# Rotary angles on GpSimd, a new order of the first loads, and the first token tile's latents ahead of the last transposes

## The chip, the cores and the metric

The kernel runs on one core of a Trainium2 chip. The metric is the device time of one execution, in microseconds (us); lower is better. The core has five engines that work in parallel, each through its own queue in order: PE (TensorE, matrix products), DVE (VectorE), ACT (ScalarE), POOL (GpSimd) and SP (SyncE, which here only issues transfers). Transfers between the chip's main memory and the on-chip memory are done by 16 DMA engines.

## The reference

One layer of a decoder block with 512 tokens of width 1024, all in float32. The normed tokens go through one wide projection, whose first columns are two low-rank latents and a rotary key; the rest feeds a differential attention and two gates.

```python
xn = rmsnorm(x, norm_mix_g[l])
proj = jnp.einsum('bsd,de->bse', xn, w_in[l])
q_lat, kv_lat, k_rope, dq, dk, dv, gate_pre = jnp.split(proj, split_idx, axis=-1)
q = jnp.einsum('bsr,re->bse', rmsnorm(q_lat, mla_q_norm_g[l]), mla_w_uq[l])
...
kv = jnp.einsum('bsr,re->bse', rmsnorm(kv_lat, mla_kv_norm_g[l]), mla_w_ukv[l])
...
o_mla = causal_attention(q_mla, k_mla, v_mla).reshape(B, S, MLA_WIDTH)
...
o_diff = rmsnorm(o1 - lam * o2, diff_subln_g[l]) * (1.0 - lambda_init)
...
x = x + jnp.einsum('bsd,de->bse', merged, w_out[l])
hn = rmsnorm(x, norm_ffn_g[l])
hid = jax.nn.silu(jnp.einsum('bsd,df->bsf', hn, w_ffn_gate[l])) * jnp.einsum('bsd,df->bsf', hn, w_ffn_up[l])
x = x + jnp.einsum('bsf,fd->bsd', hid, w_ffn_down[l])
```

Rotary turns pairs of columns by an angle, position times frequency, so a table of cosines and sines is needed for the 512 positions. The query latent has 384 columns, the other latent 256, the rotary key 32.

## The kernel before

**Two halves.** Every operand of a matrix product is split into a rounded high half and a low half (the rest), and each product is made of three (`mm3`, L298 to L302): high by high, high by low, low by high. High halves are mostly written by ACT, low halves by DVE or POOL.

**The start.** Tokens lie in four tiles x0 to x3 of 128 tokens. `LOADS` gives the order in which SP issues the first transfers: `r` small rows (gains and biases), `x0` a token tile in two column halves, `A0` a pair of query-latent weight tiles (128x384 each), `B0` a pair of tiles of the other latent with the rotary key (128x288 each), `i` the frequency column and the positions. Eight transfers can be in flight; the ninth waits for the first to land. `START` gives the order in which the preparing work is written: `r` turns the small rows into columns, `t0` transposes token tile 0 on PE (L346) and writes its gained halves (`X`, ACT L352, DVE L354), `t23` does tiles 2 and 3 together, `d6` puts six idle products on PE, `a0` and `b0` split a weight tile (L329 to L332; `W_DVE` names the tiles whose high half DVE writes in place of ACT, `W_POOL` those whose low half POOL writes in place of DVE), `s0` sums the squares of a token tile on ACT (L358).

**The latents.** `latent(0)` makes the query latents of all four token tiles, 24 products of 128x384 for each, then `latent(1)` the others, 24 of 128x288. A product tile goes from its bank (three of the kind `ps_mm`) through ACT, which squares and copies it (L448, L450). Between the third and the fourth tile of `latent(1)` stand the products that make the rotary tables (L539), from the angles.

**The angles.** L397 to L416 work out position times frequency, reduced to one turn in five steps, on DVE, on tiles of 128x128 and 128x256. Their result is `turn`; ACT makes its absolute value and eight sines (L419, L428), DVE splits those (L431, L432).

**Behind the start** come the gates, the projections of attention, the attention heads (a score step L632, a maximum on DVE L636, an exponential on ACT, transposes L658, values), the output and the FFN. Weights there go through `weights`: a raw tile (four buffers), a high half by `round_hi`, a low half by `round_lo` on the engines in `w_eng`, which is `W_ENG0` up to the first attention head's stage and `W_ENG` after it.

**What sets the order.** The program is written in one order; a scheduler then places each engine's instructions by priorities and its own model of the time, with `issue_after` as a way to hold one behind another. So a change at the start can move instructions far behind it.

Of the kernel before, what the change touches and what calls it, by code (L numbers as in the profile page):

```python
# [21 lines left out]
P = 128  # L22
# [70 lines left out]
def build(ctx, nc, tc, a, out):  # L93
# [29 lines left out]

    def dma(o, i):
        nc.sync.dma_start(out=o, in_=i)
# [21 lines left out]
    table = [nc.scalar.preload_act_table_set(LOG_EXP)]  # L147
# [24 lines left out]
    def load_x(t):  # L172
        for c in range(2):
            dma(xts[t][:, c * S:(c + 1) * S], a["x"][0, t * P:(t + 1) * P, c * S:(c + 1) * S])
# [29 lines left out]

    for step in LOADS:
        k = int(step[1:] or 0)
        if step[0] == "x":
            load_x(k)
# [49 lines left out]

    w_eng = list(W_ENG0)

    def round_hi(o, i):
        if w_eng[0] == 'act':
            nc.scalar.activation(out=o, in_=i, func=AF.Copy)  # L263
        else:
            nc.vector.tensor_copy(out=o, in_=i)  # L265
# [56 lines left out]
    last_t, last_hi = [None], [None]  # L322

    def latent_weights(b, k):
# [5 lines left out]
        else:  # L330
            nc.scalar.activation(out=w[:, 0, :], in_=raw, func=AF.Copy)
# [6 lines left out]
    def scaled_transpose(t0, t1):  # L338

        n = t1 - t0  # L340
        for k0 in range(0, KD, 4 // n):
# [11 lines left out]
            for src, hi, lo, g in parts:  # L353
                nc.vector.scalar_tensor_tensor(out=lo, in0=src, scalar=g, in1=r32(hi), op0=ALU.mult, op1=ALU.subtract)  # L354

    def x_square(t):
        with tc.issue_after(last_hi[0].ins):
            nc.scalar.activation(out=xts[t], in_=xts[t], func=AF.Square, accum_out=x_ss[:, t:t + 1])  # L358

    for step in START:  # L360
# [6 lines left out]
        elif step[0] in "ab":  # L367
            latent_weights("ab".index(step[0]), k)
        else:
            if step[0] == "s":  # L370
                x_square(k)
            else:
                scaled_transpose(k, int(step[-1]) + 1)
# [3 lines left out]

    def xa(k, sl=slice(None)):
        return [xn[k // 4][:, k % 4, s, sl] for s in range(2)]
# [6 lines left out]
    nc.vector.tensor_mul(out=lp, in0=lv[:, 0:4:2, :], in1=lv[:, 1:4:2, :])  # L386
# [14 lines left out]
    nc.vector.tensor_copy(out=ahl[:, 0, :], in_=r32(ah))  # L401
    nc.vector.tensor_sub(out=ahl[:, 1, :], in0=ang, in1=ahl[:, 0, :])
    for j, c in enumerate(_inv_2pi_pieces()):
        nc.vector.tensor_scalar(out=ry, in0=ahl, scalar1=c, scalar2=MAGIC, op0=ALU.mult, op1=ALU.add)
        nc.vector.tensor_scalar(out=ry, in0=ry, scalar1=MAGIC, scalar2=0.0, op0=ALU.subtract, op1=ALU.add)
        nc.vector.tensor_scalar(out=rx, in0=ahl, scalar1=c, scalar2=0.0, op0=ALU.mult, op1=ALU.add)
        if j == 0:
            nc.vector.tensor_sub(out=acc, in0=rx, in1=ry)
        else:
            nc.vector.tensor_sub(out=rx, in0=rx, in1=ry)  # L410
            nc.vector.tensor_add(out=acc, in0=acc, in1=rx)
    nc.vector.tensor_add(out=turn, in0=acc[:, 0, :], in1=acc[:, 1, :])
    for _ in range(2):
        nc.vector.tensor_scalar(out=ry[:, 0, :], in0=turn, scalar1=MAGIC, scalar2=0.0, op0=ALU.add, op1=ALU.add)
# [583 lines left out]
```

## Time and profile before

| what | us |
|---|---|
| median of 3 runs (764.81 to 767.35) | 766.11 |
| the profiled execution | 765.69 |
| its span in the profile | 763.9 |
| DVE busy in the span | 430.5 |
| ACT busy in the span | 293.4 |
| POOL busy in the span | 166.9 |

The profile is of one execution. A row of a timeline has the start and the length in us, the engine, the line of the kernel, the operation, what it writes and reads by the program's names, the shape, a count where equal instructions follow each other, and in brackets how long the engine stood idle before it and what ended that. Rows of a table by stretch have the stretch, its length, the busy us of PE, of PE's weight loads, of DVE, ACT and POOL, then PE's granted clock, the share of the DMA engines and GB/s.

### The profile page before, as it was taken

What the parts mean: (1) busy time and instruction counts of PE and PEld (TensorE: products, weight loads), DVE (VectorE), ACT (ScalarE), POOL (GpSimd) and SP (SyncE); (2) the same over time, 40 slices, a digit from 0 to 9 for tenths busy, and PEclk for the clock granted to TensorE, in tenths of its full rate; (3) what the DMA queues carried; (4) which work ended last, traced back from release to release, by engine and by line L of the source; (5) the groups of instructions that cost most, each with busy time, mean ns of one, the idle gap of its engine ahead of it and who ended that gap; (6) DMA issues with size and microseconds to landing.
All of it is one profiled execution on the core that took longest, in us unless ns stands there. A gap on an engine that the chain in (4) does not pass through costs nothing.

```text
span 763.9 us, 9613 instructions
## 1 busy us (share of the span) xinstructions
PE 738.9 (97%) x3639; PEld 620.5 (81%) x3639; DVE 430.5 (56%) x800; ACT 293.4 (38%) x567; POOL 166.9 (22%) x120
## 2 busy tenths in 40 slices
PE   7999999999898999999999999999999999999996
PEld 5888889887686788888889888888888888888885
DVE  6968698898999983578363333233323332213424
ACT  7464658554333421724243323222222223122314
POOL 3404343564664454430000000000000000000302
PEclk9999999999999999999999999999999999999999
DMA  9405343632422322327422332323232323232302
GB/s 305 113 1 133 88 122 88 151 85 58 108 70 69 84 83 82 111 87 254 102 83 73 94 110 83 110 83 111 83 110 83 111 83 110 85 108 84 111 0 110
DMA packets 99819, 76.72 MB, mean 100 GB/s; under 512 B 6303, under 2 KB 86973, under 8 KB 99773
## 3 DMA queue, kind: packets, MB, share of 16 engines
q1 hardware_dynamic: 99773, 76.12, 34.0%
q8 instruction: 28, 0.46, 0.2%
q14 instruction: 18, 0.15, 0.1%
HBM read 69.81 MB, written 2.10 MB: 94 GB/s over the span
## 4 chain that ended last, share of the span: by engine, by line
PE 80%; DVE 13%; issue 2%; ACT 1%; POOL 1%; DMA 1%; SPq 0%; DVEq 0%; POOLq 0%; ACTq 0%
PE ps_mm L301 22%; PE ps_mm L302 22%; PE ps_mm L300 22%; PE ps_sc L632 2%; DVE L L256 2%; PE ps_sc L300 1%; PE ps_sc L301 1%; PE ps_tr L301 1%; PE ps_tr L300 1%; PE ps_tr L302 1%; PE ps_sc L302 1%; DVE L L254 1%; PE ps_tr L658 1%; DVE w L265 1%; DVE P L684 1%
## 5 line engine op out<-in xcount | busy, mean ns | idle before, releaser
L302 PE MATMUL ps_mm<-X,w 128*128 128x512 f32 (+1 forms) x568 | 217.6, 383 | 0.0
L300 PE MATMUL ps_mm<-X,w 128*128 128x512 f32 (+1 forms) x568 | 217.3, 383 | 0.2 <-DVE t L564 0.2
L301 PE MATMUL ps_mm<-X,w 128*128 128x512 f32 (+1 forms) x568 | 217.3, 383 | 0.0
L268 DVE TENSOR_TENSOR w<-raw,w 128x1024 fp32r<-128x1024 f32 x66 | 82.3, 1248 | 161.1 <-ACT w L263 161.0
L263 ACT ACTIVATE w<-raw 128x1024 fp32r<-128x1024 f32 (+1 forms) x72 | 74.0, 1029 | 160.1 <-issue 78.9
L268 POOL TENSOR_TENSOR w<-raw,w 128x1024 fp32r<-128x1024 f32 (+3 forms) x48 | 102.5, 2139 | 118.3 <-DVE w L265 36.3
L300 PEld LDWEIGHTS ps_mm<-X,w 128*128 128x128 f32 x568 | 107.1, 189 | 20.3 <-DVE t L564 0.4
L301 PEld LDWEIGHTS ps_mm<-X,w 128*128 128x128 f32 x568 | 107.2, 189 | 19.9 <-DVE X L254 0.2
L302 PEld LDWEIGHTS ps_mm<-X,w 128*128 128x128 f32 x568 | 107.1, 189 | 20.0 <-POOL w L268 0.3
L933 POOL TENSOR_TENSOR L<-L,P 128x512 f32<-128x512 f32 (+1 forms) x9 | 11.5, 1297 | 410.2 <-ACT t L932 410.1
L155 ACT ACTIVATE P<-P,sm 128x128 f32<-128x128 f32 (+3 forms) x64 | 35.9, 561 | 60.1 <-DVE sm L636 59.9
L907 DVE TENSOR_TENSOR t<-t,ps_mm 128x512 f32<-128x512 f32 x22 | 15.1, 688 | 59.7 <-PE ps_mm L302 59.7
L632 PE MATMUL ps_sc<-L,L 96*128 96x128 f32 (+7 forms) x160 | 38.0, 334 | 8.7 <-DVE sm L636 8.6
L906 ACT ACTIVATE t<-ps_mm 128x512 f32<-128x512 f32 x22 | 13.2, 598 | 80.8 <-PE ps_mm L302 80.8
L632 PEld LDWEIGHTS ps_sc<-L,L 96*128 96x128 f32 (+1 forms) x160 | 26.1, 191 | 14.6 <-DVE sm L636 12.3
L301 PE MATMUL ps_mm<-w,L 128*128 128x512 f32 (+1 forms) x100 | 37.2, 372 | 0.0
L300 PE MATMUL ps_mm<-w,L 128*128 128x512 f32 (+1 forms) x100 | 37.2, 374 | 0.0
L302 PE MATMUL ps_mm<-w,L 128*128 128x512 f32 (+1 forms) x100 | 37.1, 373 | 0.0
L265 DVE CAST w<-raw 128x1024 fp32r<-128x1024 f32 (+3 forms) x42 | 35.9, 855 | 1.6 <-PE ps_mm L302 1.1
L250 ACT ACTIVATE L<-t 64x512 fp32r<-64x512 f32 (+2 forms) x47 | 29.1, 624 | 17.0 <-POOL t L566 7.4
L301 PE MATMUL ps_mm<-L,w 128*128 128x512 f32 x90 | 35.5, 394 | 0.0
L254 DVE TENSOR_TENSOR L<-t,L 128x512 fp32r<-128x512 f32 (+2 forms) x37 | 33.1, 896 | 4.0 <-ACT L L250 3.7
(264 smaller groups left out, 1269.0 us busy)
## 6 DMA issues: line engine op xcount, KB each, us to landing
raw<-w_in SPq DMA_DIRECT2D x28, 512.0 KB, 4.0
raw<-w_ffn_gate SPq DMA_DIRECT2D x22, 512.0 KB, 3.9
raw<-w_ffn_up SPq DMA_DIRECT2D x22, 512.0 KB, 3.9
raw<-w_ffn_down SPq DMA_DIRECT2D x22, 512.0 KB, 3.6
L<-L SPq DMA_DIRECT2D x32, 128.0 KB, 2.3
raw<-w_out SPq DMA_DIRECT2D x8, 512.0 KB, 3.6
L<-x SPq DMA_DIRECT2D x8, 256.0 KB, 5.1
raw<-w_branch_mla SPq DMA_DIRECT2D x4, 512.0 KB, 3.4
```

The source lines that it names most:

```text
L155: return nc.scalar.activation(**kw)
L250: nc.scalar.activation(out=hi, in_=src, func=AF.Copy, scale=scale)
L254: nc.vector.tensor_sub(out=lo, in0=src, in1=r32(hi))
L256: nc.vector.scalar_tensor_tensor(out=lo, in0=src, scalar=scale, in1=r32(hi), op0=ALU.mult, op1=ALU.subtract)
L263: nc.scalar.activation(out=o, in_=i, func=AF.Copy)
L265: nc.vector.tensor_copy(out=o, in_=i)
L268: (nc.vector if w_eng[1] == 'dve' else nc.gpsimd).tensor_sub(out=o, in0=i, in1=r32(hi))
L300: nc.tensor.matmul(out=o, lhsT=lh, rhs=rh, start=start, stop=False)
L301: nc.tensor.matmul(out=o, lhsT=lh, rhs=rl, start=False, stop=False)
L302: return nc.tensor.matmul(out=o, lhsT=ll, rhs=rh, start=False, stop=stop)
L632: nc.tensor.matmul(out=ps[:, :n], lhsT=q[:, i * P:n], rhs=k[:, 0:n], start=j == 0, stop=j == last)
L907: nc.vector.tensor_mul(out=g, in0=g, in1=ps)
```

## The change

Four things change in the start of the program.

- The angles, 36 instructions, are written for POOL in place of DVE.
- The first half of x0 is SP's first transfer. The small rows and the second half of x0 are issued by ACT (the `*` in `LOADS`), ahead of its table load. All of x1 and all query weights come ahead of the frequencies and positions.
- POOL writes no low half of a latent weight any more, DVE writes all of them; ACT writes the high halves but for `a0` and `a1`. The first weights behind the start (`W_ENG0`) have their low halves from DVE.
- The first token tile's query latents (`l0`) are written ahead of the transposes of tiles 2 and 3 (`t23`), which are held behind their last product. Squares of the tokens, and the splits of the other latent's weights, come later.

```diff
-LOADS = "r x0 A0 i A2 x1 A4 A6 x2 x3 B0 B2 B4 B6".split()
-START = "r t0 d6 a0 a1 a2 a3 t1 s0 s1 a4 a5 a6 a7 t23 s2 s3 b0 b1 b2 b3 b4 b5 b6 b7".split()
+LOADS = "x00 r* x01* A0 A2 x10 x11 A4 A6 i x20 x21 x30 x31 B0 B2 B4 B6".split()
+START = "r t0 d6 a0 a1 a2 a3 t1 a4 a5 a6 a7 l0 t23 s0 s1 b0 b1 b2 b3 s2 s3 b4 b5 b6 b7".split()
...
-W_POOL = "a0 a1 a4 b0 b1 b2 b3 b4 b5 b6 b7".split()
-W_DVE = "b0 b1 b2 b3 b4 b5 b6 b7".split()
+W_POOL = ()
+W_DVE = "a0 a1".split()
...
-W_ENG0 = ['act', 'pool']
+W_ENG0 = ['act', 'dve']
...
 for step in LOADS:
+        issuer[0] = nc.scalar if step[-1] == "*" else nc.sync
...
+    issuer[0] = nc.sync
+    table[0] = nc.scalar.preload_act_table_set(LOG_EXP)
...
         if w_eng[0] == 'act':
-            nc.scalar.activation(out=o, in_=i, func=AF.Copy)
+            with tc.issue_after(last_w[0].ins):
+                nc.scalar.activation(out=o, in_=i, func=AF.Copy)
...
+        elif step[0] == "a":
+            latent_weights(0, k)
+        elif step[0] == "b":
+            with tc.issue_after(last_hi[0].ins):
+                latent_weights(1, k)
+        elif step[0] == "s":
+            x_square(k)
+        elif step[0] == "l":
+            latent(0, k, k + 1)
+        elif lat_mm[0] is not None:
+            with tc.issue_after(lat_mm[0].ins):
                 scaled_transpose(k, int(step[-1]) + 1)
...
-    nc.vector.tensor_mul(out=lp, in0=lv[:, 0:4:2, :], in1=lv[:, 1:4:2, :])
+    with tc.issue_after(last_lo[0].ins):
+        nc.vector.tensor_mul(out=lp, in0=lv[:, 0:4:2, :], in1=lv[:, 1:4:2, :])
...
-    nc.vector.tensor_copy(out=ang, in_=pos_i)
-    nc.vector.tensor_scalar(out=ang, in0=ang, scalar1=ccol[:, 0:1], scalar2=0.0, op0=ALU.mult, op1=ALU.add)
-    nc.vector.tensor_copy(out=ah, in_=ang)
+    nc.gpsimd.tensor_copy(out=ang, in_=pos_i)
+    nc.gpsimd.tensor_scalar(out=ang, in0=ang, scalar1=ccol[:, 0:1], scalar2=0.0, op0=ALU.mult, op1=ALU.add)
+    nc.gpsimd.tensor_copy(out=ah, in_=ang)
...
     for j, c in enumerate(_inv_2pi_pieces()):
-        nc.vector.tensor_scalar(out=ry, in0=ahl, scalar1=c, scalar2=MAGIC, op0=ALU.mult, op1=ALU.add)
+        nc.gpsimd.tensor_scalar(out=ry, in0=ahl, scalar1=c, scalar2=MAGIC, op0=ALU.mult, op1=ALU.add)
...
-    latent(0)
+    latent(0, 1)
     latent_norm(0)
```

The rest of the angles changes in the same way, engine for engine. Lines behind the change are about 20 further on in the new file: L346 becomes L354, L300 to L302 become L308 to L310, L332 becomes L340, L354 becomes L362, L539 becomes L559, L632 becomes L652.

The order of PE where the transposes of tiles 2 and 3 stand. In the rows of before, `ps_mm_356` and `ps_mm_383` are the query latents of token tiles 0 and 1, `L_154` to `L_163` the weights of the first four of eight column blocks, and `L_69` token tile 2. Before:

```order
L301 MATMUL ps_mm_356<-L_163,X_62 128x384
L302 MATMUL ps_mm_356<-L_163,X_62 128x384
L346 MATMUL ps_tr_206<-ident,L_69 128x128
L346 MATMUL ps_sc_215<-ident,L_69 128x128
L302 MATMUL ps_mm_383<-L_154,X_62 128x384
L300 MATMUL ps_mm_383<-L_157,X_62 128x384
```

In the change `ps_mm_206` and `ps_mm_380` are these two latents, `L_200` and `L_203` the weights of the last two blocks, `L_68` and `L_69` token tiles 2 and 3:

```order
L310 MATMUL ps_mm_206<-L_200,X_62 128x384
L308 MATMUL ps_mm_206<-L_203,X_62 128x384
L309 MATMUL ps_mm_206<-L_203,X_62 128x384
L310 MATMUL ps_mm_206<-L_203,X_62 128x384
L354 MATMUL ps_tr_234<-ident,L_68 128x128
L354 MATMUL ps_tr_234<-ident,L_69 128x128
```

The first transposes of tiles 2 and 3 stood behind the fourth of eight blocks of tile 0; now they stand behind its last product.

The order of DVE behind the first token tile. `t_292` and `t_293` are tiles of the angles, `L_160`, `L_163` weights, `X_62`, `X_63` the token halves. Before:

```order
L354 SCALAR_TENSOR_TENSOR X_62<-ps_tr_122,cols,X_62 128x128 x4
L404 TENSOR_SCALAR t_293<-t_292 128x256
L406 TENSOR_SCALAR t_293<-t_292 128x256
L354 SCALAR_TENSOR_TENSOR X_63<-ps_sc_135,cols,X_63 128x128 x4
L405 TENSOR_SCALAR t_293<-t_293 128x256
L332 TENSOR_TENSOR L_160<-w_64,L_160 128x384
L332 TENSOR_TENSOR L_163<-w_64,L_163 128x384
L408 TENSOR_TENSOR t_292<-t_293 128x256
L354 SCALAR_TENSOR_TENSOR X_62<-ps_tr_166,cols,X_62 128x128 x4
```

With the change, where `L_156` to `L_165` are the first four query weights:

```order
L362 SCALAR_TENSOR_TENSOR X_61<-ps_tr_124,cols,X_61 128x128 x4
L337 CAST L_156<-w_63 128x384
L337 CAST L_159<-w_63 128x384
L362 SCALAR_TENSOR_TENSOR X_62<-ps_sc_137,cols,X_62 128x128 x4
L340 TENSOR_TENSOR L_162<-w_63,L_162 128x384
L340 TENSOR_TENSOR L_156<-w_63,L_156 128x384
L340 TENSOR_TENSOR L_159<-w_63,L_159 128x384
L340 TENSOR_TENSOR L_165<-w_63,L_165 128x384
L362 SCALAR_TENSOR_TENSOR X_61<-ps_tr_168,cols,X_61 128x128 x4
```

The angle instructions are gone from between the token halves; two high halves and two more low halves of weights stand there.

The order of PE at the first attention head, where `ps_sc` are its score steps of 128, 256 and 384 keys and `ps_mm_920` a product of the values' projection. Before, from the second step on:

```order
L632 MATMUL ps_sc_1066<-L_717,L_715 128x256 x3
L300 MATMUL ps_mm_920<-w_912,X_62 128x256
L301 MATMUL ps_mm_920<-w_912,X_62 128x256
L302 MATMUL ps_mm_920<-w_912,X_62 128x256
...
L300 MATMUL ps_mm_920<-w_917,X_63 128x256
L632 MATMUL ps_sc_1078<-L_717,L_715 128x384 x3
```

With the change:

```order
L652 MATMUL ps_sc_1066<-L_717,L_715 128x256 x3
L308 MATMUL ps_mm_920<-w_912,X_61 128x256
L652 MATMUL ps_sc_1078<-L_717,L_715 128x384 x3
L309 MATMUL ps_mm_920<-w_912,X_61 128x256
L310 MATMUL ps_mm_920<-w_912,X_61 128x256
```

Of the 13 products between the two steps 12 now stand behind the second of them. Farther on, the order of the rows in attention differs from before at most places; behind attention it is the same.

More of the change, by code (lines that the diff above doesn't have):

```diff
@@ L358, in x_square, with xa, latent @@
             nc.scalar.activation(out=xts[t], in_=xts[t], func=AF.Square, accum_out=x_ss[:, t:t + 1])
+    def xa(k, sl=slice(None)):
+        return [xn[k // 4][:, k % 4, s, sl] for s in range(2)]
+    latn = []
+    lat_ss = [sm(NB), sm(NB)]
+    lat_mm = [None]
+    def latent(b, t0=0, t1=NB):
+        c0, n, ncol = ((0, QR, QR), (QR, KVR + RD, KVR))[b]
+        for t in range(t0, t1):
+            ps = PS("pv" if t == 3 and b == 0 else "mm")
+            for k in range(KD):
+                lat_mm[0] = mm3(ps[:, :n], xa(k, slice(t * P, (t + 1) * P)), lat_w[k][b], k == 0, k == KD - 1)
+            if b == 0:
+                latn.append(LF())
+            nc.scalar.activation(out=latn[t][:, c0:c0 + ncol], in_=ps[:, :ncol], func=AF.Square,
+                                 accum_out=lat_ss[b][:, t:t + 1])
+            nc.scalar.activation(out=latn[t][:, c0:c0 + n], in_=ps[:, :n], func=AF.Copy)
     for step in START:
@@ L418, in build @@
+        nc.gpsimd.tensor_sub(out=turn, in0=turn, in1=ry[:, 0, :])
     turn_c = ry[:, 1, :]
```

64 lines of the change are left out of this document (24 added, 40 removed).

## The prediction

> **What bounds the kernel now.** I read the head of the page first, then who PE waited for, then the chain that ended last over the first 120 us, then the timelines of that stretch.
>
> ```profile
> span 763.9 us, 9613 instructions
> PE 738.9 (97%) x3639; PEld 620.5 (81%) x3639; DVE 430.5 (56%) x800; ACT 293.4 (38%) x567; POOL 166.9 (22%) x120
> ```
>
> PE is busy for 738.9 of 763.9 us. The change adds no matrix product and takes none away, so all that it can win is a part of the 25 us in which PE stands still, plus stretches where its products start late one by one. The waits of PE (total us, times, longest) say where those lie; the first four rows are from the first 120 us, the last two from 35 us to the end.
>
> ```profile
> PE ps_tr L346 <- DMA L<-x: 1.9, 1, 1.9
> PE ps_mm L301 <- DVE L L332: 1.9, 2, 1.4
> PE ps_mm L302 <- DVE X L354: 1.1, 1, 1.1
> PE ps_tr L539 <- DVE P L533: 0.6, 1, 0.6
> ...
> PE ps_sc L632 <- DVE sm L636: 8.6, 7, 1.5
> PE ps_tr L658 <- DVE P L685: 2.0, 1, 2.0
> ```
>
> The first four are in the stage that the change rewrites: tokens not yet landed, low halves of weights and tokens not yet written by VectorE, and the rotary tables' inputs. The last two, 10.6 us, lie in attention, which no line of the diff touches. The chain over the start (start, us, what) shows what the table products at 43.54 hang on:
>
> ```profile
> 3.12 4.08 DMA PT<-positions
> ...
> 17.64 1.03 DVE t L411
> ...
> 31.20 0.33 DVE t L411
> ...
> 37.38 0.30 DVE PT L416
> 37.71 0.31 ACT t L419
> ...
> 43.15 0.35 DVE P L533
> 43.54 1.19 PE ps_tr L539 x4
> ```
>
> Positions land at 7.2, the angle chain runs on VectorE to 37.68, and 5.86 us later (absolute value, table load, eight sines, splits) PE can make the tables. Between, VectorE does the angles in pieces among the low halves that PE waits for. It has no free time there:
>
> ```profile
> 25.00:30.00 5.00, 4.71 (x28) 4.39 (x26) 5.00 (x8) 0.31 (x1) 4.89 (x4) 1.00 0.00 0
> ```
>
> (length, then busy us of PE, PEld, DVE, ACT, POOL, PE clock, DMA share, GB/s): VectorE 5.00 of 5.00, in only 8 instructions.
>
> **Part 1, the loads.** Tokens 128 to 255 (the tile x1) hold PE up once:
>
> ```profile
> 4.07 0.94 SPq L125 DMA_DIRECT2D L<-x  x2
> 8.80 0.66 PE L346 MATMUL ps_tr<-ident,L 128*128 128x128 f32 x4 [1.89 <-DMA L<-x]
> 9.92 0.43 PE L300 MATMUL ps_mm<-L,X 128*128 128x384 f32 x1
> ```
>
> They are issued at 4.07 and land at 8.8. Seven issues stand ahead of them on SP, three after the change: four fewer at 0.47 (0.94 for two), 1.9 us. But all bytes ahead of them stay, less 64 KB of positions, so the transfer rate decides:
>
> ```profile
> 4.00:5.00 1.00, 1.00 (x7) 0.60 (x6) 0.34 (x2) 0.00 (x0) 0.00 (x0) 1.00 0.87 228
> 5.00:6.00 1.00, 1.00 (x9) 0.73 (x8) 0.00 (x0) 0.80 (x4) 0.00 (x0) 1.00 1.09 288
> 9.00:10.00 1.00, 0.92 (x9) 0.71 (x7) 1.00 (x2) 0.61 (x3) 0.84 (x1) 1.00 1.05 383
> ```
>
> From 4 to 6 us the queue moves 228 and 288 GB/s, later 383. Nothing gained there leaves only the positions, 64 KB at 383 GB/s, 0.2 us; full rate from 4 us would give (383 - 228 + 383 - 288) / 383 = 0.65 us more. The share of 0.87 in the first of the two rows says that part of it was missing issues. I take 0.6 us, between 0.2 and 0.85: the first latent product starts at 9.3 in place of 9.92. The Trainium skill, "DMA: Bandwidth & Descriptors", section "Issuing engines are not separate DMA queues", speaks against more: a second issuing engine only saves issue time, since all transfers share the same 16 engines. By that rule the term is 0.2; the row with 1.09 agrees with it and the one with 0.87 does not, so by the page the sum below would be 0.4 us smaller.
>
> The two issues that ScalarE now makes, and its table load behind them, cost it about as much as SP's (0.94 for two). ScalarE has nothing else to do until the first transposed tokens are there, which hides them; without that cover they would cost that 0.9 us. The lambda product that now waits for the last low half has only VectorE's weight low halves behind it, and those wait for ScalarE's high halves anyway.
>
> **Part 2, latents of the query rank.** Price of one 128x384 product: ten lie between 20.31 and 22.04, 0.173 us each; of a transpose, three between 16.26 and 16.59, 0.11 us.
>
> ```profile
> 16.26 0.49 PE L346 MATMUL ps_tr<-ident,L 128*128 128x128 f32 x3
> 16.59 0.49 PE L346 MATMUL ps_sc<-ident,L 128*128 128x128 f32 x3
> ...
> 20.31 0.34 PE L302 MATMUL ps_mm<-L,X 128*128 128x384 f32 x1
> ...
> 22.04 0.34 PE L300 MATMUL ps_mm<-L,X 128*128 128x384 f32 x1
> ...
> 33.06 0.40 PE L300 MATMUL ps_mm<-L,X 128*128 128x288 f32 x1
> ```
>
> The work is 96 x 0.173 + 16 x 0.11 = 18.4 us, and it takes from 9.92 to 33.06, 23.1 us: 4.7 us are waits and late starts. With the angles gone, VectorE's queue holds, in the new order, 8 low halves of x0, two high halves and four low halves of weights, 8 low halves of x1, and four more of weights, all at 0.26 to 0.5 us. Added up from 5.6 us, the first low half of a weight is there at 9.4 and the last of the eight at 15.5 (16 with some delay by GpSimd); PE asks for them at 9.5 and 16.4. So I leave 0.4 us of waits: this part ends at 9.3 + 18.4 + 0.4 = 28.1, against 33.06: **5.0 us earlier** with part 1. Bounds: all 4.7 us of waits kept (0.6 earlier) and none (5.4). The products of tile 0 are now all ahead of the transposes of the last 256 tokens; those need nothing but tokens landed by about 14, so nothing is queued behind a missing input there. What stands behind them on ScalarE does wait: the high halves of the last tokens now come after the square of tile 0's latents, so ScalarE idles from about 12.5 to 17, and then holds 14.7 us of work until the copy that frees the second latent bank, priced from rows such as these:
>
> ```profile
> 13.58 1.80 ACT L331 ACTIVATE L<-w 128x384 fp32r<-128x384 f32 x4
> ...
> 19.65 1.11 ACT L358 ACTIVATE L<-L 128x1024 f32<-128x1024 f32 x1
> ```
>
> That ends at 31.7; PE wants the bank one tile (3.3 us) after 28.1, at 31.4. I charge 0.3 us, between 0 and 1.7.
>
> **Part 3, latents of the other rank and the tables.** Two tiles of these take from 33.06 to the product at 39.53, 3.24 us each.
>
> ```profile
> 39.53 0.59 PE L527 MATMUL ps_sc<-t,ones 128*128 128x512 f32 x1
> ```
>
> Three tiles and that one product (about 0.5) stand before the tables: 28.1 + 10.2 + 0.3 = 38.6 for PE. The tables also need the angles, now on GpSimd, whose prices are:
>
> ```profile
> 110.64 0.37 POOL L770 TENSOR_SCALAR P<-P,sm 128x128 f32<-128x128 f32 x1 [1.78 <-DVE sm L639]
> 112.47 0.48 POOL L770 TENSOR_SCALAR P<-P,sm 128x256 f32<-128x256 f32 x1 [1.46 <-DVE sm L639]
> 126.46 0.74 POOL L268 TENSOR_TENSOR w<-raw,w 128x256 fp32r<-128x256 f32 x1 [0.29 <-POOL w L268]
> 17.59 1.76 POOL L332 TENSOR_TENSOR L<-w,L 128x288 fp32r<-128x288 f32 x2 [2.34 <-DVE L L329]
> 21.57 0.81 POOL L332 TENSOR_TENSOR L<-w,L 128x288 fp32r<-128x288 f32 x1 [0.24 <-DVE L L329]
> ```
>
> 8 one-input instructions of 128 columns at 0.37 (the casts are not in the trace on this engine; I price them alike, and at most like two-input ones, 0.2 us more in all), 15 of 256 at 0.48, 9 two-input ones of 256 at 0.74, 4 of 128 at about 0.47, and two clears at 0.49 make 19.7 us. They start when the positions land, which are now behind all eight query weight tiles, at about 10.9. Beside a busy VectorE two instructions took 1.76, one alone 0.81: 9% more. With 10% the turn is ready at 32.6 and the tables at 32.6 + 5.86 = 38.5. PE itself comes at 38.6, so the tables start at 38.6 in place of 43.54: **4.9 us gained**. The cover is 0.1 us: what GpSimd takes longer is lost one for one.
>
> **Part 4, what follows.** PE runs the same 383 matrix instructions up to the first score in both versions, so the 4.9 us carry to the scores, about 73. There the order differs: between the second and third score step stands one 128x256 product, where there were 13. In the profile the third step waits for VectorE even so:
>
> ```profile
> 78.93 0.79 PE L632 MATMUL ps_sc<-L,L 96*128 96x384 f32 x3 [1.49 <-DVE sm L636]
> ```
>
> The step starts when VectorE is done, so 12 products at 0.115 (0.173 scaled by width, an estimate) move behind it, 1.4 us, where PE has no gap to take them: I charge 1.4, between 0 (VectorE done earlier) and 1.5. Some 2.3 us of weight low halves go from GpSimd to VectorE between 54 and 62; VectorE is busy 3.15 of 5 us there:
>
> ```profile
> 55.00:60.00 5.00, 5.00 (x30) 4.13 (x29) 3.15 (x5) 2.91 (x5) 1.01 (x1) 1.00 0.15 52
> ```
>
> That hides them; without the cover they would cost up to 0.5.
>
> **Sum.** 4.9 - 1.4 = 3.5 us. The profiled execution took 765.69 (span 763.9 and 1.8 around it), so 762.2; the median shown, 766.11, is 0.4 higher, which gives 762.6.
>
> **Rivals.** *GpSimd's chain binds.* The Trainium skill, "SBUF — State Buffer", section "SBUF: two separate sides", says that VectorE and GpSimd share a port pair as an exclusive lock held for the whole instruction. By that rule, the trace agrees that one of the two stands still.
>
> VectorE's L411 at 17.64 took 1.03 us beside GpSimd's pair at 17.59, and 0.33 at 31.20 with GpSimd idle. From then to the turn VectorE has 4 + 8 + 3 weight low halves and one product to do, 7.3 us by the same rows; if each stops GpSimd in full, the turn is ready at 10.9 + 19.7 + 7.3 = 37.9 and the tables at 43.8. Then nothing of the 4.9 us is left and the 1.4 of part 4 may even cost: 766 to 767.5. For it: such collisions are in the rows. Against: in them GpSimd lost 9% and VectorE the rest.
>
> *The loads bring nothing and low halves still come late*: 0.2 us and half of part 2, 2.5, less 1.4: 764.8. For it: the transfer engines are near full in the rows above.
>
> *Better.* The score steps of the new order meet fewer blocks, so the 1.4 us do not show or more: 759 to 761.
>
> *Slower.* In attention VectorE is blocked by GpSimd's 128x1024 low halves:
>
> ```profile
> 180.12 2.38 POOL L268 TENSOR_TENSOR w<-raw,w 128x1024 fp32r<-128x1024 f32 x1 [4.44 <-DVE w L265]
> 180.43 2.61 DVE L254 TENSOR_TENSOR L<-t,L 64x512 fp32r<-64x512 f32 x1
> 183.50 0.62 PE L632 MATMUL ps_sc<-L,L 128*128 128x384 f32 x2 [1.48 <-DVE sm L636]
> ```
>
> A 64x512 piece beside one took 2.61 us and PE then stood 1.48. Eight such waits make the 10.6 us. The order of scores, weights and fills in attention is dealt anew, and each further hit costs 1.3 us. From 5 more on (6.5 - 3.5 = 3.0 us) the kernel is slower: 767 to 770. For it: PE's rows in attention stand in another order nearly throughout. Against: the number of such low halves is the same.
>
> **How the numbers follow.** A measurement of this kernel can tell about 0.3%, 2.3 us. Forecast 0.45 (faster); better 0.12 (faster); GpSimd's chain binds 0.18 (faster 0.03, same 0.14, slower 0.01); loads and low halves 0.10 (faster 0.02, same 0.08); more blocks 0.15 (same 0.04, slower 0.11). Together faster 0.62, same 0.26, slower 0.12. The range goes from 766.1 less the upper bounds (5.4 and two blocks fewer, 2.6), 758.1, to the binding chain with the 1.4 us lost, 767.5; outside lie about 0.1 of the slower case and a little of the better one.
>
> **What would show it.** In the new profile: first 128x384 product near 9.3; the 128x288 products from about 28; GpSimd's last L452 at 32 to 33 and no PE wait above 0.5 us at the table products near 38.6; a wait of up to 2.9 us at the third score step. A table wait of 2 us or more puts GpSimd's chain right; equal times at 75 us and a later end put the blocks in attention right. Casts from integers much above 0.37 us on GpSimd, or a late second queue, would make the forecast wrong.

## The result, and the profile after

The change makes the kernel slower: 777.82 us (median of 4 runs, 776.45 to 778.63) against 765.60 for the kernel of before on the same chip, a ratio of 1.0158 with a 95% interval of 1.0139 to 1.0176. The prediction was 762.6, with a range up to 767.5. So it was wrong in sign and in range.

The head of the page of the profiled execution after the change (776.45 us, span 774.3):

```profile
span 774.3 us, 9593 instructions
PE 745.0 (96%) x3639; PEld 625.8 (81%) x3639; DVE 426.7 (55%) x775; ACT 293.9 (38%) x573; POOL 173.2 (22%) x139
```

The span grew by 10.4 us, PE's busy time by only 6.1, although PE has the same 3639 products. PE stands still longer, and part of its products take longer. Who PE waited for in the change (total us, times, longest), first rows:

```profile
PE ps_sc L652 <- DVE sm L656: 8.5, 6, 3.7
PE ps_tr L559 <- DVE P L553: 4.4, 1, 4.4
PE ps_tr L723 <- DVE L L715: 3.4, 1, 3.4
PE ps_sc L354 <- DMA L<-x: 1.9, 1, 1.9
```

Against before, the wait at the tables (L559) is 4.4 us in place of 0.6, the longest at the scores (L652) is 3.7 in place of 1.5, and one late in attention (L723) is new. The rows of PE's timeline that answer to the steps of the prediction:

```profile
7.14 0.66 PE L354 MATMUL ps_sc<-ident,L 128*128 128x128 f32 x4 [1.86 <-DMA L<-x]
11.40 0.60 PE L308 MATMUL ps_mm<-L,X 128*128 128x384 f32 x2
...
29.89 0.29 PE L308 MATMUL ps_mm<-L,X 128*128 128x288 f32 x1
...
45.11 1.86 PE L559 MATMUL ps_tr<-P,P 128*128 128x512 f32 x4 [4.37 <-DVE P L553]
...
83.69 1.33 PE L652 MATMUL ps_sc<-L,L 96*128 96x384 f32 x3 [3.67 <-DVE sm L656]
```

The first latent product is 1.5 us late (11.40 against 9.92). The first 128x288 product is 3.2 early (29.89 against 33.06), so the latents gained 4.7 on the way. The tables are 1.6 late (45.11 against 43.54), the third score step 4.8 late (83.69 against 78.93).

**Where along the way the time goes.** Since the order of PE's products differs, I compare at equal work. The widths of PE's products, without the idle ones on zeros, are added up along the trace. For the last product that the kernel of before has started at a given time, I look up when the other kernel has as much behind it. The table gives that difference in us (minus is ahead; the different order alone makes some tenths of it, and more at 200 in the six kernels whose attention stands in another order). At 400 it agrees within 0.4 with the difference of the two spans. The rows below the first are the experiments of the next section. Some figures in their expectations come from a coarser count, such as 9.4 us behind at 90 us for the change, where this one has 8.6.

| kernel | 35 | 50 | 60 | 70 | 85 | 200 | 400 |
|---|---|---|---|---|---|---|---|
| the change | -3.3 | +2.3 | +3.1 | +3.1 | +8.6 | +8.4 | +10.4 |
| mulform | -3.5 | -0.9 | +0.2 | +0.2 | +5.3 | +5.1 | +7.2 |
| u_angles | -3.6 | -3.8 | -2.7 | -2.7 | +3.0 | +2.7 | +4.8 |
| u_weng0 | -4.0 | +6.9 | +6.9 | +7.0 | +7.0 | +7.0 | +6.9 |
| x01_sp | -4.0 | +3.2 | +3.9 | +4.0 | +9.7 | +9.4 | +11.5 |
| b_weng0 | -0.9 | -1.6 | -1.5 | -1.4 | +3.7 | +3.5 | +5.5 |
| warm | -3.0 | +2.1 | +3.1 | +3.1 | +8.4 | +8.1 | +10.1 |
| best1 | -4.0 | -0.4 | +0.7 | +0.7 | +0.7 | +0.7 | +0.7 |
| best2 | -4.3 | -0.6 | +0.5 | +0.5 | +0.5 | +0.5 | -0.8 |
| h3 | -4.5 | -4.7 | -3.7 | -3.6 | -2.1 | -2.1 | -2.2 |
| h3_start | +0.6 | +0.2 | +0.2 | +0.2 | +1.7 | +1.8 | +0.5 |
| h3_loads | -0.2 | -0.4 | +0.7 | +0.7 | +0.7 | +0.7 | +0.7 |
| h3_pool | -4.0 | +0.8 | +1.9 | +1.9 | +1.9 | +2.0 | +1.9 |

The change is 3.3 us ahead at 35 us, and loses in two places: 5.6 us between 35 and 50 us, at the tables, and 5.5 between 70 and 85, at the third score step. The rest of attention adds 1.8 more. The two places have different causes.

**The tables.** GpSimd's groups between 10 and 40 us (count, busy us, mean ns; the last number is its idle time before them), and the last instruction of its chain from the timeline:

```profile
L441 POOL TENSOR_SCALAR t<-t 128x256 f32<-128x256 f32 x5 | 5.7, 1144 | 0.3
...
L440 POOL TENSOR_SCALAR t<-t 128x256 f32<-128x256 f32 x5 | 2.2, 443 | 0.4
L451 POOL TENSOR_SCALAR t<-t 128x128 f32<-128x128 f32 x2 | 1.4, 690 | 0.2
L450 POOL TENSOR_SCALAR t<-PT 128x128 f32<-128x128 f32 x2 | 1.3, 647 | 0.2
...
L433 POOL CAST PT<-PT 128x128 f32<-128x128 int32 x1 | 0.6, 571 | 9.5 <-DMA PT<-positions 9.5
```

```profile
38.50 0.46 POOL L452 TENSOR_TENSOR PT<-PT,t 128x128 f32<-128x128 f32 x1
```

The chain runs from 11.59 to 38.96, 27.4 us. L440 and L441 have the same shape, one input and two operations with constants; L440 (multiply, add) takes 443 ns, L441 (subtract, add) 1144. From 38.96 the rest needs its 6.15 us, and the tables start at 45.11.

**The third score step.** VectorE has no gap of over 0.5 us from 59.48 to 84 us. Three low halves stand in its queue that GpSimd made before (2.46 us together), and two casts are stretched beside GpSimd:

```profile
59.48 0.55 DVE L276 TENSOR_TENSOR w<-raw,w 128x384 fp32r<-128x384 f32 x1
...
64.19 1.23 DVE L276 TENSOR_TENSOR w<-raw,w 128x1024 fp32r<-128x1024 f32 x1
...
66.06 0.68 DVE L276 TENSOR_TENSOR w<-raw,w 128x512 fp32r<-128x512 f32 x1
...
78.28 2.52 DVE L273 CAST w<-raw 128x1024 fp32r<-128x1024 f32 x1
...
81.33 2.10 DVE L273 CAST w<-raw 128x384 fp32r<-128x384 f32 x1
83.35 0.27 DVE L656 CUSTOM_DVE_ANT_0 P<-ps_sc,mask 128x128 f32<-128x128 f32 x1
```

The maximum at 83.35 is what the third step waits for. The two long casts are nothing new: the kernel of before has them in the same place, at 2.00 and 2.20 us.

The rows split the 5.5 us that are lost here into three parts. PE is 3.1 us behind at 70 us and the step starts 4.76 late, so VectorE's longer queue costs about 1.65. The 12 products that stood ahead of the step, 0.12 us each, come behind it now: 1.4. And behind the wait PE runs at half the clock. Two of its 128x256 products behind the step, in the change:

```profile
84.82 0.41 PE L309 MATMUL ps_mm<-w,X 128*128 128x256 f32 x1
85.03 0.41 PE L310 MATMUL ps_mm<-w,X 128*128 128x256 f32 x1
```

and in the kernel of before:

```profile
79.94 0.28 PE L301 MATMUL ps_mm<-w,X 128*128 128x256 f32 x1
80.05 0.28 PE L302 MATMUL ps_mm<-w,X 128*128 128x256 f32 x1
```

They follow each other at 0.21 us in place of 0.12, 24 of them, until 89.87; with the step itself (1.13 us to the next product in place of 0.81) that is 2.5 us, the largest of the three.

**The clock.** The table by stretch (length, busy us of PE, PE's weight loads, VectorE, ScalarE, GpSimd, then PE's granted clock) shows that second price of a pause. Before the change PE had 1.00 in all of the first 150 us. In the change:

```profile
5.00:10.00 5.00, 3.14 (x14) 1.57 (x13) 2.99 (x12) 3.10 (x10) 0.00 (x0) 0.78 1.03 361
10.00:15.00 5.00, 5.00 (x30) 5.00 (x29) 4.75 (x15) 3.82 (x12) 2.92 (x7) 0.87 1.07 384
...
45.00:50.00 5.00, 4.89 (x22) 4.50 (x23) 3.80 (x15) 1.91 (x9) 0.00 (x0) 0.66 0.00 0
...
80.00:90.00 10.00, 6.33 (x30) 6.31 (x30) 6.91 (x15) 4.08 (x10) 4.45 (x5) 0.66 0.73 205
```

After the pause of 4.4 us the 128x288 products follow each other at 0.24 us in place of 0.13, until 48.7. The Trainium skill, "TensorE: Matmul & The Clock Gate", section "Part 1: The HAM clock gate", says that an idle window of about 3.4 us halves the clock until PE has been busy for another one. This trace agrees in the length: 0.66 over 5 us is half the clock for 3.4 us, and 0.66 over 10 us, at the third score step, is 6.8 us, twice that. It does not agree in the idle time that it takes: 0.78 and 0.87 from 5 to 15 us are half the clock for about 3.4 us again, behind a wait of only 1.86.

### The profile page after: what moved, and what is told of

Read it like the earlier page. It is cut to its first block, busy times and chain, and to the rows that moved or that the text cites. A ratio compares the mean times of both kernels' runs of the same rounds, so it can differ in the third digit from the quotient of the medians.

```text
span 774.3 us, 9593 instructions
## 1 busy us (share of the span) xinstructions
PE 745.0 (96%) x3639; PEld 625.8 (81%) x3639; DVE 426.7 (55%) x775; ACT 293.9 (38%) x573; POOL 173.2 (22%) x139
## 4 chain that ended last, share of the span: by engine, by line
PE 74%; DVE 15%; POOL 4%; issue 4%; ACT 3%; DMA 1%; DVEq 0%; POOLq 0%
PE ps_mm L308 20%; PE ps_mm L309 20%; PE ps_mm L310 20%; DVE w L273 2%; DVE P L656 2%; DVE L L262 2%; DVE P L705 2%; ACT P L157 1%; DVE P L704 1%; PE ps_sc L652 1%; DVE L L260 1%; PE ps_sc L308 1%; PE ps_sc L309 1%; PE ps_tr L309 1%; PE ps_tr L308 1%
## 5 line engine op out<-in xcount | busy, mean ns | idle before, releaser
L308 PE MATMUL ps_mm<-X,w 128*128 128x512 f32 (+1 forms) x568 | 217.7, 384 | 0.3 <-DVE L L507 0.3
L310 PE MATMUL ps_mm<-X,w 128*128 128x512 f32 (+1 forms) x568 | 217.5, 383 | 0.0
L276 DVE TENSOR_TENSOR w<-raw,w 128x1024 fp32r<-128x1024 f32 (+1 forms) x72 | 88.0, 1226 | 161.2 <-ACT w L271 161.0
L308 PEld LDWEIGHTS ps_mm<-X,w 128*128 128x128 f32 x568 | 107.2, 189 | 20.9 <-DVE L L507 0.7
L276 POOL TENSOR_TENSOR w<-raw,w 128x1024 fp32r<-128x1024 f32 (+3 forms) x42 | 93.5, 2226 | 136.2 <-DVE w L273 90.3
L310 PEld LDWEIGHTS ps_mm<-X,w 128*128 128x128 f32 x568 | 107.2, 189 | 19.5
L953 POOL TENSOR_TENSOR L<-L,P 128x512 f32<-128x512 f32 (+1 forms) x9 | 11.5, 1295 | 409.9 <-ACT t L952 409.9
L652 PE MATMUL ps_sc<-L,L 96*128 96x128 f32 (+7 forms) x160 | 39.3, 337 | 8.6 <-DVE sm L656 8.5
L273 DVE CAST w<-raw 128x1024 fp32r<-128x1024 f32 (+3 forms) x42 | 38.6, 918 | 0.9 <-PE ps_mm L310 0.7
L652 PEld LDWEIGHTS ps_sc<-L,L 96*128 96x128 f32 (+1 forms) x160 | 26.7, 192 | 14.5 <-DVE sm L656 11.5
L310 PE MATMUL ps_mm<-w,L 128*128 128x512 f32 (+1 forms) x100 | 37.2, 374 | 0.0
L308 PE MATMUL ps_mm<-w,L 128*128 128x512 f32 (+1 forms) x100 | 37.2, 373 | 0.0
L309 PE MATMUL ps_mm<-L,w 128*128 128x512 f32 x90 | 35.5, 395 | 0.0
L308 PE MATMUL ps_mm<-L,w 128*128 128x512 f32 x90 | 35.3, 394 | 0.0
L310 PE MATMUL ps_mm<-L,w 128*128 128x512 f32 x90 | 35.1, 390 | 0.0
```

What stands on the lines that cost most here:

```text
L276: (nc.vector if w_eng[1] == 'dve' else nc.gpsimd).tensor_sub(out=o, in0=i, in1=r32(hi))
L308: nc.tensor.matmul(out=o, lhsT=lh, rhs=rh, start=start, stop=False)
L309: nc.tensor.matmul(out=o, lhsT=lh, rhs=rl, start=False, stop=False)
L310: return nc.tensor.matmul(out=o, lhsT=ll, rhs=rh, start=False, stop=stop)
L652: nc.tensor.matmul(out=ps[:, :n], lhsT=q[:, i * P:n], rhs=k[:, 0:n], start=j == 0, stop=j == last)
```

## The experiments

Each kernel is the change, or the kernel of before, with a short edit. Times are medians; the kernel of before ran beside them, at 766.27 us (first four), 766.02 (next four) and 765.16 (last four).

| kernel | us | ratio to before, 95% interval |
|---|---|---|
| mulform | 775.05 | 1.0120 (1.0091 to 1.0149) |
| u_angles | 769.97 | 1.0046 (1.0030 to 1.0063) |
| u_weng0 | 773.50 | 1.0096 (1.0074 to 1.0117) |
| x01_sp | 777.83 | 1.0152 (1.0137 to 1.0167) |
| best1 | 768.46 | 1.0021 (1.0009 to 1.0033) |
| best2 | 765.60 | 0.9996 (0.9981 to 1.0010) |
| b_weng0 | 771.45 | 1.0067 (1.0053 to 1.0081) |
| warm | 776.77 | 1.0130 (1.0108 to 1.0152) |
| h3 | 763.56 | 0.9978 (0.9969 to 0.9988) |
| h3_start | 766.38 | 1.0017 (1.0008 to 1.0025) |
| h3_loads | 767.25 | 1.0026 (1.0017 to 1.0035) |
| h3_pool | 769.10 | 1.0053 (1.0035 to 1.0071) |

### mulform: the price of GpSimd's additions

```diff
-        nc.gpsimd.tensor_scalar(out=ry, in0=ry, scalar1=MAGIC, scalar2=0.0, op0=ALU.subtract, op1=ALU.add)
+        nc.gpsimd.tensor_scalar(out=ry, in0=ry, scalar1=1.0, scalar2=-MAGIC, op0=ALU.mult, op1=ALU.add)
...
```

L450 and L451 are rewritten in the same way.

> The change with GpSimd's additions and subtractions of the constant written as a multiplication by 1 with the addition behind it; same numbers. Theory A (the form sets the price): in the change L441, which begins with a subtraction, takes 1.07 to 1.27 us, L440, which begins with a multiplication, 0.41 on the same 128x256. Each L441 then takes about 0.41 and each 128-wide L450 and L451 about 0.37 in place of 0.65 to 0.73; the chain is 4.7 us shorter and ends at about 34.3, the table products start when PE gets there (40.6) in place of 45.11, with a wait under 0.5, and the half clock from 45 to 49 is gone: 4.5 + 1.6 = 6.1 us less, 771.7. Rival B (VectorE beside it, or the dependence on the instruction before, sets the price): L441 stays near 1.1, time 777.8 within 1.

GpSimd's groups, ScalarE's row for the absolute value, and PE's next wait, in mulform:

```profile
L441 POOL TENSOR_SCALAR t<-t 128x256 f32<-128x256 f32 x5 | 2.3, 464 | 0.3
```

```profile
34.55 0.31 ACT L455 ACTIVATE t<-PT 128x128 f32<-128x128 f32 x1 [2.71 <-POOL PT L452]
...
36.07 0.40 PE L308 MATMUL ps_mm<-L,X 128*128 128x288 f32 x1 [3.04 <-ACT L L389]
```

The price is settled: 464 ns in place of 1144 for the same subtraction, and the chain ends at 34.5, as expected. But only 2.8 of the expected 6.1 us came by the medians. In this kernel the absolute value stands ahead of the copies that free the latent banks in ScalarE's queue, so ScalarE waits 2.71 us for GpSimd and PE 3.04 for ScalarE, at 36 in place of 45. The tables start at 43.43. GpSimd's chain still ends last, one engine further on.

### u_angles: the angles back on VectorE

```diff
-    nc.gpsimd.tensor_copy(out=ang, in_=pos_i)
+    nc.vector.tensor_copy(out=ang, in_=pos_i)
...
```

All 36 instructions go back; all else is as in the change.

> The change with the 36 angle instructions on VectorE again, all else as in the change. Theory A (GpSimd's chain holds the tables up): VectorE is busy 6.2, 7.4 and 7.3 of 10 us between 10 and 40, so 36 instructions at 0.2 to 0.35 us, 10 us, fit; the turn is there before 34, the tables start near 40.6 without a wait above 0.5, no half clock behind them: about 771.7. Rival B (VectorE's low halves come late again as before the change): query latents end above 31.5 in place of 29.9, tables at 43 or later, 774 or more.

The tables in u_angles, on PE:

```profile
40.27 1.10 PE L559 MATMUL ps_tr<-P,P 128*128 128x512 f32 x4
```

No wait and no half clock here: the expectation held, and the time fell by 7.85 us (777.82 to 769.97), 5.7 between the two profiled spans. The latents stay early, at 3.6 us ahead at 35 us. So their gain never needed the angles to leave VectorE. The third score step takes as much as in the change: 2.7 us ahead at 70, 3.0 behind at 85.

### u_weng0 and b_weng0: who writes the first weights' low halves

```diff
-W_ENG0 = ['act', 'dve']
+W_ENG0 = ['act', 'pool']
```

> The change with the low halves of the first weights behind the start on GpSimd again (W_ENG0). Between the second and third score step then stand 13 products again in place of 1. Theory A (the third score step is lost by this part): tables at 45.1 as in the change, the third step waits 1.5 in place of 3.7, no half clock from 80 to 90, and PE, which is 9.4 us behind the kernel of before at 90 us in the change, is 3.3 to 4.5 behind: about 772.5. Rival B (the third step is late only because VectorE's whole work comes later): wait still above 3, time within 1 of 777.8.

PE's two waits in u_weng0:

```profile
49.13 1.22 PE L559 MATMUL ps_tr<-P,P 128*128 128x512 f32 x2 [7.28 <-DVE P L553]
...
85.87 0.79 PE L652 MATMUL ps_sc<-L,L 96*128 96x384 f32 x3 [1.48 <-DVE sm L656]
```

Theory A held at the scores: the wait is 1.48, and nothing is lost from 70 to 85 us (+7.0 at both), with a clock of 1.00 there. It missed at the tables, where I expected no difference: 3 of these low halves now stand among GpSimd's angles (3.35 us at 35.01 and 0.72 at 38.74), and the tables come 4 us later than in the change. So the total fell by 4.3, not 5.3.

The reverse alone, in the kernel of before (`['act', 'pool']` to `['act', 'dve']`):

> The kernel of before with one word changed: the low halves of the first weights behind the start on VectorE (W_ENG0 of the change). Between the second and third score step stands 1 product in place of 13. Theory A (this part alone loses the third step and deals the attention anew): level with before up to 65 us, wait of 3.7 at the third step, then half the clock, 5.6 behind at 90 us, and 7.7 at the end, as in the change with the angles on VectorE (2.5 ahead, then 3.1, then 5.2 behind): 774. Rival B (it costs this only where the start comes late or is dealt anew): within 1.5 of 766.3.

```profile
79.18 1.33 PE L632 MATMUL ps_sc<-L,L 96*128 96x384 f32 x3 [3.65 <-DVE sm L636]
```

One word costs 5.4 us in the kernel of before. From 70 to 85 us it loses 5.1, about as much as the change does, and by the same three parts: the step starts 0.25 later than before where PE had been 1.4 ahead, 12 products come behind it, and 20 products follow at 0.21 us. I had expected it to start level; it is 1.6 ahead at 50 us, the larger part of the 2.5 us by which it ends better than the 774 I gave. The same VectorE instruction in the kernel of before and in b_weng0 shows one source of that lead:

```profile
26.74 2.45 DVE L386 TENSOR_TENSOR PT<-PT 128x128 f32<-128x128 f32 x1
```

```profile
26.02 0.28 DVE L386 TENSOR_TENSOR PT<-PT 128x128 f32<-128x128 f32 x1
```

In the kernel of before GpSimd writes three low halves there (4.29 us from 26.64 on), and VectorE stands in one small instruction for 2.45 us. The new wait late in attention (3.4, L723 in the change) is in all six kernels with this setting and in none of the others. These six lose 1.7 to 1.9 us between 85 and 400 us; of the others none loses any. So this setting also costs some 1.8 us in attention.

### x01_sp: the second queue

```diff
-LOADS = "x00 r* x01* A0 A2 x10 x11 A4 A6 i x20 x21 x30 x31 B0 B2 B4 B6".split()
+LOADS = "x00 r* x01 A0 A2 x10 x11 A4 A6 i x20 x21 x30 x31 B0 B2 B4 B6".split()
```

> The change with the second half of the first token tile issued by SP right behind the first half; only the small rows are left on ScalarE's queue. Theory A (the second queue brings this half late, and PE's pause brings the half clock of the start): it lands near 5 in place of 7, the first 128x384 product starts at 9.5 to 10 in place of 11.40, query latents end at 28.0 to 28.6 in place of 29.9. Since the tables wait for GpSimd, whose start hangs on the positions, they stay at 45.1 and the time stays at 777.8 within 1. Rival B (a gain at the start carries through): 776.3 or less. Rival C (the transfer rate alone decides): the half lands at 7 again and nothing moves.

```profile
5.79 0.66 PE L354 MATMUL ps_sc<-ident,L 128*128 128x128 f32 x4
...
9.76 0.60 PE L308 MATMUL ps_mm<-L,X 128*128 128x384 f32 x2
...
45.47 2.07 PE L559 MATMUL ps_tr<-P,P 128*128 128x512 f32 x4 [5.50 <-DVE P L553]
```

Theory A in all points. Issued at 1.43 by ScalarE, while SP issues weights and x1 from 1.18 on, this half reached PE at 7.14; issued by SP right behind the first half it is there by 5.79, and the latents start 1.64 earlier. Most of that is the clock: in u_angles, which loads as the change does, the half reached PE as late, at 7.43, after a wait of 1.56, but the clock stayed at 1.00 and the first 128x384 product stood at 10.02. The tables wait for GpSimd and swallow it: the wait is 5.50, the time unchanged.

### warm: the clock by itself

```diff
+    with tc.issue_after(lat_mm[0].ins):
+        dummies(14, still)
```

> The change with 14 products of 128x512 on zeros, 3.1 us, ahead of the product of the ones (L547), where PE would come to the tables too early; PE's pause at the tables shrinks from 4.4 to about 1.3 us. The tables hang on GpSimd and start at 45.1 as before. Theory A (a pause of PE of over 3 us brings half the clock): the clock stays 1.00 from 45 to 50, and PE, 3.3 us behind the kernel of before at 60 us in the change, is 1.7 behind; at the third score step VectorE binds, and what is left of the 1.6 there decides between 776.2 and 777.8. Rival B (the clock follows something else): 0.66 again in that stretch, 777.8.

The two stretches around the tables in warm:

```profile
40.00:45.00 5.00, 4.08 (x27) 3.37 (x25) 1.76 (x4) 4.48 (x11) 0.34 (x1) 1.00 0.00 0
45.00:50.00 5.00, 3.79 (x24) 3.29 (x24) 4.64 (x17) 3.37 (x12) 0.00 (x0) 1.00 0.00 0
```

At the tables it went as Theory A says: with a pause of 2.05 us in place of 4.37 the clock stays at 1.00. The 24 products of 128x288 behind the first tables take 3.27 us in place of 4.12, those four table products 1.26 in place of 1.66, so the half clock cost 1.25 us here. PE is 3.1 us behind at 60 us all the same, since GpSimd's chain ended 1.4 us later in this run (40.34) and the tables started at 46.13, 1.0 later than I had expected. So the total of 776.77 says little; the two rows and the products say it. That 3 us are the limit is not shown: a wait of 2.28 us at the start of this same run is followed by 0.73 and 0.93 from 5 to 15 us.

### best1 and best2: both causes taken out

best1 is u_angles with `W_ENG0` of before; best2 is best1 with the loads of x01_sp.

> The change with the angles on VectorE and the first weights' low halves (W_ENG0) on GpSimd again; left of it are the new loads, the splits of the latent weights without GpSimd, and the first tile's latents ahead. Theory A (the parts add): with the angles on VectorE alone PE was 2.5 us ahead of the kernel of before at 60 us, and the third score step then lost 5.6; with W_ENG0 undone there was no loss at that step. So 2.5 ahead at 90 us and at the end: 763.7. Rival B (GpSimd's low halves stop VectorE, which now has the angles as well): tables late, 766 or more.

> As best1, and the second half of the first token tile issued by SP. Theory A (the start now carries through, since nothing behind it waits for GpSimd): the first 128x384 product starts near 9.9 in place of 11.4; x01_sp was 0.75 us ahead of the change from 30 to 40 us, so 0.7 less than best1: 763.0. Rival B: the tables or scores take it up again, same as best1 within 0.3.

Theory A failed in both; in best1 its rival B came true. The third step loses nothing, as expected, but the tables wait 2.4 to 2.5 us, and half the clock follows (0.74 from 40 to 45 us in best2). By the medians best2 is 2.9 us better than best1, where 0.7 was expected; by the table 0.2 of it is there at 85 us and 1.5 at 400. Why the rest comes in attention is open. VectorE and GpSimd in best2 at that place:

```profile
30.48 2.37 DVE L452 TENSOR_TENSOR PT<-PT,t 128x128 f32<-128x128 f32 x1
32.88 0.93 DVE L450 TENSOR_SCALAR t<-PT 128x128 f32<-128x128 f32 x1
```

```profile
30.08 4.34 POOL L276 TENSOR_TENSOR w<-raw,w 128x1024 fp32r<-128x1024 f32 x3 [27.10 <-ACT w L271]
```

Beside GpSimd's three low halves L452 takes 2.37 us (0.29 in u_angles) and L450 0.93 (0.22). The Trainium skill, "SBUF — State Buffer", section "SBUF: two separate sides", has this as a port pair that one of the two holds for a whole instruction; the rows agree.

### h3: the first three low halves on VectorE, the next three on GpSimd

```diff
+        n_lo[0] += 1
-        (nc.vector if w_eng[1] == 'dve' else
+        (nc.vector if w_eng[1] == 'dve' and not 3 < n_lo[0] <= 6 else
```

Besides that it has the angles on VectorE and the loads of x01_sp.

> The change with the angles on VectorE, the second half of the first token tile issued by SP, and of the six first weights behind the start the low halves of the first three on VectorE and of the next three on GpSimd. Theory A (in best2 the wait of 2.4 us at the tables came from GpSimd's three low halves from 30.1 to 34.4 us, beside which one angle instruction took 2.37 us in place of 0.29): the tables start near 39.5 without a wait above 0.5, PE is 4.2 us ahead of the kernel of before at 50 us, 2.5 to 3 at 60, and the third score step, with 13 products ahead of it, takes nothing back: 763.3. Rival B (VectorE binds the scores whatever comes before): the lead is gone at 85 us, 765.6 as best2.

```profile
28.66 0.29 PE L310 MATMUL ps_mm<-L,X 128*128 128x288 f32 x1
...
39.38 1.09 PE L561 MATMUL ps_tr<-P,P 128*128 128x512 f32 x4
...
75.28 0.79 PE L654 MATMUL ps_sc<-L,L 96*128 96x384 f32 x3 [1.49 <-DVE sm L658]
```

The tables start at 39.38 without a wait and PE is 4.7 us ahead at 50 us. The third step waits 1.49, as before the change, yet 1.5 of the lead goes there, with a clock of 0.66 from 75 to 80 us; 2.1 us remain to the end of the profiled run, 1.6 by the medians. At 763.56 us h3 beats both kernels, by 0.12 to 0.31% against before. Why the clock falls there is open.

### h3_start, h3_loads, h3_pool: what each other part is worth

h3_start has the `START` of before, h3_loads the transfers in the order of before, all on SP, h3_pool the angles on GpSimd in the multiplied form.

> As h3, but with the preparing work in the order of before (START), so the first token tile's latents come behind all transposes. Theory A (the lead at the latents is from this order): first 128x288 product at 31 or later in place of 29.1, lead at 40 us 2 us smaller than h3's, 765. Rival B (the lead is from the loads and from VectorE's and ScalarE's split of the weights): same as h3 within 0.5 at 40 us and at the end.

> As h3, but with the transfers in the order of before and all on SP (rows first, frequencies and positions ahead of the second token tile). Theory A (the prediction's first term): the first 128x384 product starts 0.6 us later than in h3, and so does all up to the tables: 0.6 us more than h3. Rival B: only the transfer rate counts, same within 0.2.

> As h3, but with the angles on GpSimd in the form that begins with a multiplication. Theory A (GpSimd's chain still ends last, at 34.5, and ScalarE's copies of latent banks stand behind the absolute value of it): PE waits about 3 us near 36 as in mulform, tables at 42 to 43 in place of 39.5, 2.5 to 3 us more than h3. Rival B (with the prices of the multiplied form GpSimd is as good a place): same as h3 within 0.5, or better since VectorE is free.

The waits of PE in the first 50 us that are new against h3, in this order:

```profile
12.74 0.48 PE L356 MATMUL ps_tr<-ident,L 128*128 128x128 f32 x1 [2.02 <-DMA L<-x]
...
33.66 0.40 PE L310 MATMUL ps_mm<-L,X 128*128 128x288 f32 x1 [1.05 <-ACT L L391]
```

```profile
13.22 0.44 PE L311 MATMUL ps_mm<-L,X 128*128 128x384 f32 x1 [1.88 <-DVE L L342]
```

```profile
36.41 0.40 PE L310 MATMUL ps_mm<-L,X 128*128 128x288 f32 x1 [3.86 <-ACT L L391]
```

Without the new order of preparing, transposes wait for tokens that the new loads bring later. Without the new loads, the low halves of the weights come late. Both waits are followed by half the clock for about 3.4 us (0.78 and 0.88 in h3_start, 0.88 and 0.78 in h3_loads, from 10 to 20 us). Either part undone takes the whole lead at 35 us (+0.6 and -0.2), so the two are worth it only together. The 0.6 us that I gave to the loads was near for the first 128x384 product (10.74 in h3_loads, 9.97 in h3), but their worth is 3.7 us by the medians, through the low halves. The angles on GpSimd cost 5.5 us even at the better price, by the way that mulform showed: the tables start at 45.25, later than the 42 to 43 expected, since the wait of 3.86 is followed by half the clock (0.68 from 35 to 40 us).

## Why the prediction was wrong

- **What bounds the kernel.** Right in that products wait at the start for loads, low halves and angles. Wrong in the reading of VectorE's 5.00 of 5.00 us in 8 instructions: that was not a full engine. One of the eight was the L386 above, 2.45 us for 0.28. A busy time in few instructions beside a busy GpSimd is waiting, and taking GpSimd's low halves away frees VectorE without moving the angles.
- **Part 1, first latent product at 9.3, 0.6 us gained.** Wrong in sign, 11.40: I counted the issues saved and the bytes ahead for x1, and took the half tile on the second queue to be as early as on the first. It came over 1.3 us later, and PE's pause for it was followed by a clock of 0.78 from 5 to 10 us; the clock is the larger part (10.02 with the same loads in u_angles, where it stayed at 1.00). x01_sp undoes it (9.76), and shows that it did not matter for the time while the tables wait for GpSimd.
- **Part 2, the latents.** Right. They take 29.89 - 11.40 = 18.5 us against 18.4 and 0.4 of waits; in h3 they end at 28.66, against the forecast 28.1. The reason given was wrong: I let the angles' leaving VectorE pay for it, and u_angles has the same lead with the angles on VectorE. So the size came out right in part by luck.
- **Part 3, GpSimd's chain of 19.7 us and 10%.** This step failed. The instructions alone took 24.8 us and 2.5 lay between them, 27.4 in place of 21.7. Of the 5.1 us more, 3.3 are L441 (five at 1.14, priced 0.48), 1.2 the one-input instructions of 128 columns, 0.6 the rest. I had priced instructions that begin with a subtraction or an addition from rows that multiply. The sentence on the cover was right: GpSimd's chain ended 6.4 us later than forecast (38.96 against 32.6, 0.7 of it by a later start) and the tables came 6.5 later. PE itself was ready at 40.74, 2.1 later than the 38.6 that I gave it, so even without the wait only 2.8 of the 4.9 us would have been there.
- **Part 4, 1.4 us at the third score step, and low halves of 2.3 us hidden.** This step failed too. I looked for the low halves at 54 to 62 us, where VectorE had room (3.15 of 5 us); they stand at 59 to 67, in a queue that was already 9.04 of 10 us busy between 60 and 70. The 1.4 us for the 12 products was right, but the step came 1.65 later through VectorE, which I had put at nothing, and half the clock behind the wait, which no term of the sum had, cost 2.5. Alone the setting cost 5.1 us there (b_weng0). No run moves the low halves without the products: the setting moves both, and the split is read from the rows.
- **The rivals.** GpSimd's chain binding was right, at a chance of 0.18, with tables at 43.8 (45.1 measured). The way I gave, VectorE stopping GpSimd, was not it; GpSimd's own price was. The slower rival, more blocks in attention, was a small part: attention behind the third step adds 1.8 of the 10.4 us. No rival had the two losses together, and none had the clock.

The sum then reads, from the medians: 777.82 for the change; 7.85 less with the angles on VectorE (u_angles), 4.3 less with the low halves on GpSimd (u_weng0). The two do not simply add, since the low halves on GpSimd hold up the angles on either engine: both undone give 768.46 (best1), with x01 on SP as well 765.60 (best2), level with before; and 763.56 (h3) when GpSimd's low halves also stay out of the angles' way. The forecast was 762.6: the gain of the new order of loads and preparing was there, and the two moves of work between VectorE and GpSimd took it and 12 us more.

## What to carry to other kernels

A chain that moves to another engine is to be priced operation by operation, by rows with the same first operation, and each microsecond of error counts fully where the cover is a tenth of one. Work is hidden only in the stretch in which it will really stand, so its place is read from the new order before its cover is read from the trace. A wait can cost more than its length, through the clock behind it. When several edits come in one change, run each alone: here two were worth some 3 to 4 us, but only together, and two others took 12.

## What the hardware showed that I had not expected

- GpSimd's one-input instruction with two constants takes 0.44 us on 128x256 when it begins with a multiplication, 1.14 when it begins with a subtraction; written as a multiplication by 1 the latter takes 0.46. On 128x128 it took 0.65 when it began with an addition and 0.37 with a multiplication (L450 and L434 in the change).
- A pause of PE of 4.4 us brings half the clock for 3.4 us, one of 2.0 (warm) did not. In h3 a wait of 1.49 was followed by 0.66 from 75 to 80 us, and the same wait of 1.49 before the change was not; one of 1.86 at the start of the change was, one of 3.04 in mulform was not. So the length of the wait alone does not decide, and what does no run shows.
- A transfer of 256 KB issued at 1.43 us on a second queue reached PE at 7.14; on the first queue, issued right behind its other half, by 5.79. Whether the queue or the weights that SP issued around it made it late, no run tells apart.
